# Second pass of a down projection: other places for a norm's chain, for gate weights and for embedding loads

## The chip, the core and the metric

One core of a Trainium2 chip runs the whole program. The metric is the device time of one execution in microseconds; the time before is the median of three runs, 795.0 us (793.97 to 795.13). The engines are TensorE (PE, which multiplies matrices), VectorE (DVE), ScalarE (ACT), GpSimd (POOL), and SyncE, whose queue (SP) issues the loads. Each engine takes its instructions in the order in which they were laid down for it.

## The reference

One layer of a hybrid model on 512 tokens of width 1024, in float32: a state-space mixer and a sparse attention side by side, their merge, a convolutional feed-forward block, a gated per-layer embedding, and a final norm. What matters here is the end:

```python
h = h + conv_ffn(rmsnorm(h, g_ffn[i]), w_up[i], conv_w[i], conv_b[i], w_down[i])
gate = jax.nn.sigmoid(rmsnorm(h, g_ple[i]) @ w_ple_gate[i])
h = h + gate * (p[i] @ w_ple_proj[i])
return rmsnorm(h, g_final)
```

`conv_ffn` ends in a product of a hidden 512 x 2816 with `w_down`, 2816 x 1024: the down projection. `rmsnorm(h, g_ple)` is called norm 3 below. `p @ w_ple_proj`, the embedding, does not depend on the rest; the kernel computes it at its start and parks it in DRAM (`pjd`), in eight pieces of 128 tokens by 512 columns.

## The kernel before

**Products.** Every float32 operand of a product is split into a high and a low part in a reduced format (`split`: ACT copies the high part, DVE or POOL subtracts it from the source to get the low one), and each product is three matmuls, high x high, high x low and low x high (`mm3`, lines 82 to 84).

**The down projection.** The hidden's 22 blocks of 128 rows are taken in 11 pairs. Pair 0 is done plainly. Pairs 1 to 10 (`for c in range(NR, NP)`) go through a scheme with seven half-size products in place of eight: the tokens are cut into halves of 256, the output into halves of 512 columns, and sums of weight blocks and of hidden blocks are multiplied. A *first pass* over the ten pairs does products 2, 1, 6 and 5. A *second pass* does product 3, two pairs at a time (`third(0)` to `third(4)`, twelve matmuls each), and then, per pair, products 4 and 7 (`fourth(c)`, twelve matmuls). The results are added onto the residual `hres` by DVE (`onto`). `sums_c(c)` loads sums of weights that were parked in DRAM (`ue`, 512 KB), and ACT and DVE split them into `uh`, `ul`, which have four places: pair c + 4 takes that of pair c once `fourth(c)` is done. `split_sums(1)` splits a pair's hidden sums for `fourth`.

**What else stands in the second pass.** `third(4)` completes product 3, so that DVE can complete the first 256 tokens of `hres`. These get norm 3 there: `squared_half` (ACT, sums of squares), `normed(0)` (ten small DVE operations that take the reciprocal root, then the scaling into `xn` on DVE and ACT), and `transposed(0, ...)`, a generator of two steps: each does eight transposes on PE, four copies on ACT (high parts `n`) and four operations on DVE (low parts `n`, line 63). The gate's weights are loaded and split as well: `gate_part(c)` for the first 512 output columns (`wg0`), `other_gate(c)` for the second (`wg1`), each c a fourth of the 1024 rows, 512 KB. `embedding(i)` loads the four parked pieces of column half i into `pj`.

**The gate** follows: eight groups of 24 matmuls into `pg`, in the order of tokens (0, 1) for column half 0, then half 1, then tokens (2, 3) for half 0 and half 1. The second token half's norm (`normed(1)`) is written at the end of the second pass, its two steps of transposes stand before the third and the fourth group. `sgt` is the tanh of a group and `gated_sum` puts gate and embedding onto `hres`. `g4` is the final gain, loaded and then scaled by POOL.

**Order.** In the second pass, up to `written.close()` (line 1841), the order of PE, SP, ACT and DVE is the order of the code. Behind it PE and SP keep the code's order and the others are ordered by a planner that simulates the program.

**Buffers.** Tiles come from `Slot`: 18 small ones of 512 columns (S0 to S17) and 22 big ones of 1024 (B0 to B21), in two lists of free slots. A new tile takes the slot that has been free longest; its first writer waits until the last reader of the tile that had the slot is done. `done()` puts a slot back. When no small slot is free, a big one is cut in two. Besides, `wraw` without a place of its own takes a buffer from a ring of three (tag `wr`), which the raw weights of the first pass, of `third` and of the gate share:

```python
if raw is None:
    raw = pw.tile([P, kt * c], F32, name="wr", tag="wr", bufs=3)
```

The second pass before the change, cut to its order:

```python
for c in range(NR, NP):
    if c == NR + 1:
        third(4)
        turned = transposed(0, normed(0, sns[0]))
    if c >= NP - 2:
        next(turned)
    fourth(c)
    n = c - NR
```

Of the kernel before, what the change touches and what calls it, by code (L numbers as in the profile page):

```python
# [18 lines left out]
P = 128  # L19
T = 512  # L20
NQ = T // P
D = 1024
# [22 lines left out]
def hybrid_kernel(ctx: ExitStack, tc: tile.TileContext, A, out):  # L45
# [3 lines left out]
    def dr(name, off, ap):  # L49
        t = A[name]  # L50
        return bass.AP(tensor=t.tensor, offset=t.offset + off, ap=ap)

    def tt(o, a, b, op, e=V):
        e.tensor_tensor(o, a, b, op=op)  # L54
# [19 lines left out]
    def copy(o, a):  # L74
        S.activation(o, a, AF.Copy)  # L75

    def split(hi, lo, src, e=V):
        copy(hi, src)
        tt(lo, src, hi, SUB, e)
# [20 lines left out]
    def bank(tag, name):  # L100
        return psp.tile([P, 512], F32, tag=tag, name=name, bufs=BANKS[tag])
# [80 lines left out]
    def wraw(name, ld, row0, c0, kt, c, raw=None):  # L182

        if raw is None:
            raw = pw.tile([P, kt * c], F32, name="wr", tag="wr", bufs=3)
            raw = raw.rearrange("p (k c) -> p k c", k=kt)
        n = (row0 // (kt * P)) * (ld // c) + c0 // c
        nc.sync.dma_start(raw, dr(name, n * P * kt * c, [[kt * c, P], [c, kt], [1, c]]))
        return raw

    def wload(name, ld, row0, c0, kt, c, e=V, keep=None, raw=None):
        if raw is None:
            raw = wraw(name, ld, row0, c0, kt, c)
        if keep is None:
            hi = pw.tile([P, kt * c], F32R, name="wh", tag="wh").rearrange("p (k c) -> p k c", k=kt)
            lo = pw.tile([P, kt * c], F32R, name="wl", tag="wl").rearrange("p (k c) -> p k c", k=kt)
        else:
            hi, lo = keep
        split(hi, lo, raw, e)
        return hi, lo  # L200
# [507 lines left out]
    for lv in range(5):  # L708
        n = 1 << lv
# [33 lines left out]
    with tc.issue_after(zero_at):  # L743
        for t in (*ZZ[0], *CX[0], *ZZ[1], *CX[1]):
            n = t.shape[1] * t.shape[2] * t.shape[3] * t.shape[4] // 8
# [297 lines left out]
    for hc in range(2):  # L1043
# [3 lines left out]
        for cc in range(2):  # L1047
            c = 2 * hc + cc
# [15 lines left out]
    class Unit:  # L1064
# [40 lines left out]
        def transposed(self, kt):  # L1105
            w = T - kt * P
            ps = bank("t", "ptp")
            for qt in range(kt, NQ):
                PE.transpose(ps[:, (qt - kt) * P:(qt - kt + 1) * P],  # L1109
                             self.pr[qt][:, kt * P:(kt + 1) * P], ident)  # L1110
            self.ph[kt], self.pl[kt] = (pt.tile([P, T], F32R, name=n, tag=n, bufs=3)[:, :w] for n in ("ph", "pl"))
            split(self.ph[kt], self.pl[kt], ps[:, :w])
# [331 lines left out]
    NP = NF // 2  # L1444
    NR = 1
# [102 lines left out]
    def sums_split(c, n, x):  # L1548
        t = Slot("ue", 2)
        nc.sync.dma_start(t.parts(), sums[c][2 * n:2 * n + 2].rearrange("n p c -> p n c"))  # L1550
        split(uh[:, x], ul[:, x], t.parts())
        t.done()

    park_at = [2, 4, 6, 8, 9, 11, 13, 14, 16, 18]
    for f in range(NF):
# [6 lines left out]
        for ab in range(2):  # L1562
            keep = [kept[2 * ab + x].parts(KD) for x in range(2)] if kept else None
# [22 lines left out]
    with tc.manual_schedule(engines={mybir.EngineType.PE, mybir.EngineType.SP}):  # L1586
# [7 lines left out]
        def sums_c(c):  # L1594
            sums_split(c, 1, (c - NP) % NSET)
# [45 lines left out]
        def product(n, c, lhs, rhs, js=(0, 1)):  # L1641
            for j in js:
                x = slice(j * P, (j + 1) * P)
                mm3(acc[n][j], lhs[0][:, x], lhs[1][:, x], rhs[0], rhs[1], c == NR and n != 2, c == NP - 1, n == 2)
# [6 lines left out]

        n3w = 2

        def gate_part(c):

            raw = wraw("w_ple_gate", D, 2 * c * P, 0, 2, 512)
            for k in range(2):
                wg0.append([Slot(f"wg0{x}", 1, F32R).t for x in "hl"])
                split(*wg0[-1], raw[:, k])

        def embedding(i):

            for qt in range(NQ):
                pjs[i, qt] = Slot("pj", 1).t
                nc.sync.dma_start(pjs[i, qt], pjd[i, qt])

# [62 lines left out]
        def third(x):  # L1729
            w, own = third_w.pop(x)  # L1730
            for i, c in enumerate(thirds[x]):
                product(3, c, hid[c].S4, (w[0][:, i], w[1][:, i]))
                for t in hid[c].split14:
                    t.done()
            for t in own:
                t.done()
# [11 lines left out]
        def squared_half(qp, sn, i, js=(0, 1)):  # L1748
            for j in js:
                S.activation(pw.tile([P, 512], F32, name="sq", tag="mg"), halves(hres[:, 2 * qp + j])[i], AF.Square,  # L1750
                             accum_out=sn[:, 2 * i + j:2 * i + j + 1])
# [4 lines left out]
        def normed(qp, sn):  # L1756
            xns = [[Slot("xn", 1) for _ in range(2)] for _ in range(2)]
            tt(sn[:, 0:2], sn[:, 0:2], sn[:, 2:4], ADD)
            r = rstd_of(sn[:, 0:2], n=2)
            for j in range(2):  # L1760
                scaled([t.t for t in xns[j]], halves(hres[:, 2 * qp + j]), r[:, j:j + 1])
            return xns
# [25 lines left out]
        sns = [sn_of(0), sn_of(1)]  # L1788
        wg1 = []

        def other_gate(c):
            wg1.append([Slot(f"wg1{x}", 2, F32R).parts() for x in "hl"])
            wload("w_ple_gate", D, 2 * c * P, 512, 2, 512, keep=wg1[-1])

        squared_half(0, sns[0], 0)
        third(0)
        third_weights(3)
        third(1)
# [4 lines left out]
        third_weights(4)  # L1803
        third(2)
        third(3)
        sums_c(NR + 3)
        for j in range(2):
            onto(j, D1, u5s[:, j])
        hid[NP - 4].split_sums(1)
        for c in range(NR, NP):  # L1810
            if c == NR + 1:
                third(4)
                for j in range(2):
                    onto(j, D1, acc[3][j])
                squared_half(0, sns[0], 1)
                for j in range(2):
                    onto(2 + j, D0, u2s[:, j])
                    onto(2 + j, D1, u5s[:, j])
                u2.done()
                u5.done()  # L1820
                turned = transposed(0, normed(0, sns[0]))
            if c >= NP - 2:
                next(turned)
            fourth(c)
            n = c - NR
            if c + 4 < NP:
                sums_c(c + 4)
            if n == 0:
                gate_part(1)
                other_gate(0)  # L1830
                other_gate(1)
            if n < 3:
                hid[NP - 3 + n].split_sums(1)
            if n in (3, 5):
                gate_part(2 + (n - 3) // 2)
            if n in (4, 6):
                embedding((n - 4) // 2)
                other_gate(n // 2)
        WG.append(lambda x, k: wg0[k][x])
        turned = transposed(1, normed(1, sns[1]))  # L1840
        written.close()
        WG.append(lambda x, k: wg1[k // 2][x][:, k % 2])

# [1 line left out]
        sg4 = Slot("g4", 2)  # L1845
        g4 = sg4.t
        nc.sync.dma_start(g4, dr("g_final", 0, [[0, P], [1, D]]))
        sgs = [Slot("sgt", 1) for _ in range(2)]
        sgn = [0]
        ts(g4, g4, math.sqrt(D), e=G)  # L1850
        ss = [pf.tile([P, 8], F32, name=f"ssf{qt}") for qt in range(NQ)]
# [163 lines left out]
```

## Time and profile before

| | |
|---|---|
| median of the runs | 795.0 us (793.97 to 795.13) |
| profiled execution: its time | 795.69 us |
| its span, first to last instruction | 794.0 us |
| PE busy | 777.7 us, 98% of the span |
| DVE, ACT, POOL busy | 563.5, 416.5, 250.1 us |
| PE clock granted, mean | 0.995 |

In rows of the trace the columns are start, duration, engine, line, operation, output<-inputs, shapes and count; in brackets stands how long the engine had been idle before and what released it. A row with a count over one merges neighbours of one kind. SP rows are the issuing of loads; the time from there until the data is in place is called landing. Names are those of buffers, and where two tiles shared a buffer, one can be shown under the other's name (`wg0l` for a hidden sum, `pj` for an `xn`). Matmul rows overlap, so PE's pace is read from start to start.

### The profile page before, as it was taken

How to read it: one execution, taken by the hardware profiler on the slowest of the kernel's cores; microseconds unless marked ns; L12 is line 12 of the kernel's file. 1: busy time of each engine (PE TensorE's matmuls, PEld its weight loads, DVE VectorE, ACT ScalarE, POOL GpSimd, SP SyncE). 2: the span in 40 equal slices, each digit the busy share in tenths (PEclk: the TensorE clock that was granted, in tenths of full speed). 3: DMA queues.
4: the chain of work that ended last, by engine and by line, in shares of the span. 5: the costliest groups of instructions: out<-in, count | busy, mean ns of one | idle time of the engine just before them, and what ended most of it. 6: DMA issues, size and time to landing. Idle time of an engine off the chain costs nothing.

```text
span 794.0 us, 12256 instructions
## 1 busy us (share of the span) xinstructions
PE 777.7 (98%) x4404; PEld 655.7 (83%) x4404; DVE 563.5 (71%) x1137; ACT 416.5 (52%) x757; POOL 250.1 (32%) x298
## 2 busy tenths in 40 slices
PE   9999999999999999999999999999999999999896
PEld 8887878888888888888998888888888888887685
DVE  6987999766677639798675566665664776876743
ACT  6836645657777654445644344344344446645532
POOL 3577433136465534001123332333332300000221
PEclk9999999999999999999999999999999999999899
DMA  8954121423234136201155566566544275576011
GB/s 345 362 158 148 60 88 47 141 72 114 55 107 157 56 125 247 96 11 54 36 189 200 206 206 229 186 237 209 194 151 133 106 273 207 172 280 209 0 54 54
DMA packets 44333, 118.59 MB, mean 149 GB/s; under 512 B 5360, under 2 KB 7792, under 8 KB 44272
## 3 DMA queue, kind: packets, MB, share of 16 engines
q1 hardware_dynamic: 43696, 116.75, 43.0%
q10 hardware_dynamic: 576, 1.05, 0.4%
q8 instruction: 35, 0.57, 0.3%
q14 instruction: 26, 0.21, 0.1%
HBM read 97.86 MB, written 15.73 MB: 143 GB/s over the span
## 4 chain that ended last, share of the span: by engine, by line
PE 89%; DVE 6%; ACT 2%; issue 2%; DMA 1%; POOL 0%; POOLq 0%; ACTq 0%; SPq 0%; DVEq 0%
PE pj L82 6%; PE pj L83 5%; PE pj L84 5%; PE ua L83 5%; PE ua L82 5%; PE ub L83 5%; PE ub L82 5%; PE ua L84 5%; PE ub L84 5%; PE p L84 3%; PE p L82 3%; PE p L83 3%; PE sps L1089 2%; PE ptp L1109 2%; PE br L82 2%; PE br L84 2%
## 5 line engine op out<-in xcount | busy, mean ns | idle before, releaser
L54 POOL TENSOR_TENSOR wl<-wr,wh 128x1024 fp32r<-128x1024 f32 x45 | 109.6, 2435 | 285.8 <-ACT wh L75 279.0
L75 ACT ACTIVATE wh<-wr 128x1024 fp32r<-128x1024 f32 x96 | 101.4, 1057 | 91.0 <-issue 34.8
L82 PE MATMUL pj<-n1h,wh 128*128 128x512 f32 x224 | 90.9, 406 | 0.4 <-DVE QT L54 0.4
L83 PE MATMUL pj<-n1l,wh 128*128 128x512 f32 x224 | 87.9, 392 | 0.0
L84 PE MATMUL pj<-n1h,wl 128*128 128x512 f32 x224 | 87.7, 392 | 0.0
L54 DVE TENSOR_TENSOR wl<-wr,wh 128x1024 fp32r<-128x1024 f32 x51 | 62.8, 1231 | 32.7 <-ACT wh L75 32.7
L63 DVE SCALAR_TENSOR_TENSOR cv<-ub,cols,cv 128x511 f32<-128x511 f32 (+1 forms) x44 | 33.0, 749 | 48.1 <-ACT cv L1511 47.3
L83 PE MATMUL ua<-n2l,wh 128*128 128x512 f32 (+1 forms) x168 | 64.6, 385 | 0.0
L82 PE MATMUL ua<-n2h,wh 128*128 128x512 f32 (+1 forms) x168 | 64.6, 385 | 0.0
L84 PE MATMUL ua<-n2h,wl 128*128 128x512 f32 (+1 forms) x168 | 64.5, 384 | 0.0
L84 PE MATMUL ub<-n2h,wl 128*128 128x512 f32 (+1 forms) x168 | 64.5, 384 | 0.0
L82 PE MATMUL ub<-n2h,wh 128*128 128x512 f32 (+1 forms) x168 | 64.5, 384 | 0.0
L83 PE MATMUL ub<-n2l,wh 128*128 128x512 f32 (+1 forms) x168 | 64.5, 384 | 0.0
L84 PEld LDWEIGHTS pj<-n1h,wl 128*128 128x128 f32 x224 | 42.1, 188 | 8.9
L82 PEld LDWEIGHTS pj<-n1h,wh 128*128 128x128 f32 x224 | 42.1, 188 | 8.3 <-DVE QT L54 0.9
L83 PEld LDWEIGHTS pj<-n1l,wh 128*128 128x128 f32 x224 | 42.2, 188 | 7.4 <-issue 0.2
L60 POOL TENSOR_SCALAR pr<-pr,su,gates 128x512 f32<-128x512 f32 (+2 forms) x64 | 38.7, 616 | 16.5 <-DVE su L1101 16.1
L75 ACT ACTIVATE ph<-ptp 128x128 fp32r<-128x128 f32 (+1 forms) x64 | 27.9, 436 | 26.1 <-PE ptp L1109 25.9
L54 DVE TENSOR_TENSOR pl<-ptp,ph 128x128 fp32r<-128x128 f32 (+1 forms) x64 | 31.1, 486 | 14.3 <-ACT ph L75 13.3
L1100 ACT ACTIVATE pr<-pr,nb 128x512 f32<-128x512 f32 (+2 forms) x64 | 35.5, 558 | 3.0 <-DVE nb L1098 2.9
L82 PEld LDWEIGHTS ub<-n2h,wh 128*128 128x128 f32 x168 | 31.6, 188 | 6.3
L84 PEld LDWEIGHTS ua<-n2h,wl 128*128 128x128 f32 x168 | 31.6, 188 | 6.3
(499 smaller groups left out, 2036.1 us busy)
## 6 DMA issues: line engine op xcount, KB each, us to landing
wr<-in_w_up_dram SPq DMA_DIRECT2D x44, 512.0 KB, 3.8
wr<-in_w_in_dram SPq DMA_DIRECT2D x28, 512.0 KB, 4.0
b<-in_w_down_dram SPq DMA_DIRECT2D x20, 512.0 KB, 5.5
bs<-b SPq DMA_DIRECT2D x40, 256.0 KB, 3.1
ue<-bs SPq DMA_DIRECT2D x20, 512.0 KB, 5.2
wr<-in_w_down_dram SPq DMA_DIRECT2D x12, 512.0 KB, 4.0
QQ<-QT SPq DMA_DIRECT2D x16, 256.0 KB, 4.6
xs<-in_w_out_dram SPq DMA_DIRECT2D x8, 512.0 KB, 8.3
```

What stands on the lines that cost most here:

```text
L54: e.tensor_tensor(o, a, b, op=op)
L60: e.tensor_scalar(o, a, s1, s2, op0=op0, op1=op1)
L63: e.scalar_tensor_tensor(o, a, s, b, op0=op0, op1=op1)
L75: S.activation(o, a, AF.Copy)
L82: PE.matmul(ps, lh, rh, start=start, stop=False, skip_group_check=goes_on)
L83: PE.matmul(ps, lh, rl, start=False, stop=False, skip_group_check=goes_on)
L84: PE.matmul(ps, ll, rh, start=False, stop=stop, skip_group_check=goes_on)
L1089: PE.matmul(o, self.QQ[:, x, qt * P:(qt + 1) * P], KK[:, :, self.g, :w] if both else KK[:, self.br, self.g, :w], start=x == 0, stop=x == 1)
L1100: S.activation(pp, pp, AF.Exp, bias=nb, scale=-1.0, accum_out=su)
L1109: PE.transpose(ps[:, (qt - kt) * P:(qt - kt + 1) * P], self.pr[qt][:, kt * P:(kt + 1) * P], ident)
```

## The change

Raw gate weights get slots of their own (`gate_raw`, one big slot each, given back after the split) in place of the ring. `gate_part(1)` and `other_gate(0)` move ahead of the loop over `fourth`; `other_gate(1)` stays in step 0; `normed(0)` moves from step 1, ahead of `fourth(2)`, to the end of step 2; the first `squared_half` moves behind `third(3)`; `other_gate(2)` moves from step 4 to step 6 and `other_gate(3)` from step 6 to step 8, behind the first step of transposes and `fourth(9)`. Of the eight embedding loads, two stay in the pass (step 6, behind `other_gate(2)`), six go behind `normed(1)`, ahead of the final gain's load. The two `sgt` slots are taken earlier, ahead of those six.

```diff
+        def gate_raw(c, i):
+            s_ = Slot("gr", 2)
+            return s_, wraw("w_ple_gate", D, 2 * c * P, i * 512, 2, 512, raw=s_.parts())
+
         def gate_part(c):
-
-            raw = wraw("w_ple_gate", D, 2 * c * P, 0, 2, 512)
+            s_, raw = gate_raw(c, 0)
             for k in range(2):
                 wg0.append([Slot(f"wg0{x}", 1, F32R).t for x in "hl"])
                 split(*wg0[-1], raw[:, k])
-
-        def embedding(i):
-
-            for qt in range(NQ):
+            s_.done()
+
+        def embedding(i, qts):
+
+            for qt in qts:
                 pjs[i, qt] = Slot("pj", 1).t
                 nc.sync.dma_start(pjs[i, qt], pjd[i, qt])
...
         def other_gate(c):
+            s_, raw = gate_raw(c, 1)
             wg1.append([Slot(f"wg1{x}", 2, F32R).parts() for x in "hl"])
-            wload("w_ple_gate", D, 2 * c * P, 512, 2, 512, keep=wg1[-1])
-
-        squared_half(0, sns[0], 0)
+            split(*wg1[-1], raw)
+            s_.done()
+
         third(0)
         third_weights(3)
...
         third(2)
         third(3)
+        squared_half(0, sns[0], 0)
+        gate_part(1)
         sums_c(NR + 3)
+        other_gate(0)
...
-        for c in range(NR, NP):
-            if c == NR + 1:
+        for n, c in enumerate(range(NR, NP)):
+            if n == 1:
                 third(4)
...
-                turned = transposed(0, normed(0, sns[0]))
             if c >= NP - 2:
                 next(turned)
             fourth(c)
-            n = c - NR
             if c + 4 < NP:
                 sums_c(c + 4)
-            if n == 0:
-                gate_part(1)
-                other_gate(0)
-                other_gate(1)
             if n < 3:
                 hid[NP - 3 + n].split_sums(1)
+            if n == 0:
+                other_gate(1)
+            if n == 2:
+                turned = transposed(0, normed(0, sns[0]))
             if n in (3, 5):
                 gate_part(2 + (n - 3) // 2)
-            if n in (4, 6):
-                embedding((n - 4) // 2)
-                other_gate(n // 2)
+            if n == 6:
+                other_gate(2)
+                embedding(0, range(2))
+            if n == 8:
+                other_gate(3)
         WG.append(lambda x, k: wg0[k][x])
         turned = transposed(1, normed(1, sns[1]))
+        sgs = [Slot("sgt", 1) for _ in range(2)]
+        embedding(1, range(2))
+        for i in range(2):
+            embedding(i, range(2, NQ))
         written.close()
```

More of the change, by code (lines that the diff above doesn't have):

```diff
@@ L1847, in hybrid_kernel @@
         nc.sync.dma_start(g4, dr("g_final", 0, [[0, P], [1, D]]))
-        sgs = [Slot("sgt", 1) for _ in range(2)]
         sgn = [0]
```

## The prediction

> **What bounds the kernel now.** I read the page's engine shares, then all waits of TensorE (PE), then the last hundred microseconds in stretches, then the instructions of PE, ScalarE (ACT), VectorE (DVE) and the DMA queue (SP) in order of time around the two places that came up. First the page's share and the longest wait of PE in the whole execution (total, times, longest):
>
> ```profile
> PE 777.7 (98%) x4404; PEld 655.7 (83%) x4404; DVE 563.5 (71%) x1137; ACT 416.5 (52%) x757; POOL 250.1 (32%) x298
> ...
> PE pg L82 <- DVE n L63: 3.5, 1, 3.5
> ```
>
> PE is busy 98% of the span, so time can come back only where PE waits or runs slowly. The longest wait is for the second pass's follower, the gate (`pg`). Stretches of time around it (length; busy time and instructions of PE, its weight loads, DVE, ACT and POOL; PE clock, DMA share, GB/s):
>
> ```profile
> 734.71:738.41 3.70, 0.16 (x2) 0.03 (x1) 3.70 (x8) 2.86 (x8) 3.33 (x1) 0.90 0.00 0
> 738.41:744.73 6.32, 6.32 (x15) 5.00 (x16) 4.90 (x11) 2.67 (x8) 0.14 (x1) 0.52 0.00 0
> ```
>
> Behind the second pass PE stands for 3.70 us, and then runs 6.3 us at a clock of 0.52. No DMA moves then. PE's own instructions:
>
> ```profile
> 714.54 0.39 PE L82 MATMUL p<-uh,ffsh 128*128 128x512 f32 x1
> ...
> 717.03 0.39 PE L84 MATMUL p<-uh,ffsh 128*128 128x512 f32 x1
> 718.08 0.50 PE L82 MATMUL p<-uh,wg0l 128*128 128x512 f32 x1 [0.66 <-ACT uh L75]
> 719.34 0.50 PE L83 MATMUL p<-ul,wg0l 128*128 128x512 f32 x1 [0.76 <-DVE ul L54]
> 719.68 0.40 PE L84 MATMUL p<-uh,ffsl 128*128 128x512 f32 x1
> ...
> 724.73 0.39 PE L82 MATMUL p<-uh,ffsh 128*128 128x512 f32 x1
> ...
> 734.48 0.39 PE L84 MATMUL p<-uh,ffsl 128*128 128x512 f32 x1
> 738.41 0.77 PE L82 MATMUL pg<-wg0h,n 128*128 128x512 f32 x1 [3.54 <-DVE n L63]
> ...
> 744.50 0.40 PE L84 MATMUL pg<-wg0h,n 128*128 128x512 f32 x1
> ```
>
> From 714.54 to 717.03 are eleven steps, 0.226 us each: full rate. Call `fourth(c)` f(c); each is twelve steps, 2.72 us. f(6)'s third matmul was due at 717.26 + 0.45 = 717.71 and ran at 719.68: **1.97 us lost**. The gate's first matmul was due at 734.71 and ran at 738.41: **3.70 lost**. The next fourteen steps, to 744.50, took 6.09 instead of 3.17: **2.92 lost**. Together 8.59 us that the change could return; elsewhere in the pass PE keeps its pace.
>
> Why PE waited, on ACT (four rows), DVE (three) and SP (two):
>
> ```profile
> 715.74 1.34 ACT L148 ACTIVATE xn<-hres,ry 128x512 f32<-128x512 f32 x2 [3.46 <-DVE ry L63]
> 716.99 1.04 ACT L75 ACTIVATE uh<-ue 128x1024 fp32r<-128x1024 f32 x1
> ...
> 733.59 1.06 ACT L75 ACTIVATE wg1h<-wr 128x1024 fp32r<-128x1024 f32 x1 [7.69 <-DMA wr<-in_w_ple_gate_dram]
> 734.56 3.01 ACT L169 ACTIVATE n<-nt,cols 128x256 fp32r<-128x256 f32 x8
> ...
> 711.37 2.49 DVE L54 TENSOR_TENSOR hres<-hres,u 128x512 f32<-128x512 f32 x4
> 713.78 0.15 DVE L54 TENSOR_TENSOR ssn<-ssn 128x2 f32<-128x2 f32 x1
> ...
> 735.83 3.22 DVE L63 SCALAR_TENSOR_TENSOR n<-nt,cols,n 128x256 fp32r<-128x256 f32 x8
> ...
> 724.92 2.78 SPq L1665 DMA_DIRECT2D pj<-pjd  x4
> 727.80 0.38 SPq L188 DMA_DIRECT2D wr<-in_w_ple_gate_dram  x1
> ```
>
> First place: f(6)'s high part `uh` (716.99) stands on ACT behind `normed(0)`'s `xn`, which waited 3.46 us for the norm's chain on DVE. Second place: `other_gate(3)`'s split waited 7.69 us for its load, and all eight copies `n` of norm 3's transposed rows stood behind it. The load left SP only at 727.80, behind four embedding loads. PE went on 0.13 us after the sixth low part (735.83 + 6 x 0.40 = 738.28).
>
> **The change, part by part.** All times below are on the clock of before; without the first stall each f starts 1.97 earlier: f(8) at 724.73 - 1.97 = 722.76, f(7) 2.72 before it at 720.04, the end of the pass E at 734.71 - 1.97 = 732.74. f(10) starts 2.72 before that, at 730.0; two groups of transposes share the 1.8 left between the end of f(8) and f(10) beside f(9), which starts at 726.4.
>
> *Norm 3's chain, one step later.* No instruction is added. On ACT and DVE the order becomes: the adds after `third(4)`, two squares, the split for f(6), that of hidden pair 9, f(7), pair 10, then the chain, then f(8). `gate_part(1)` and `other_gate(0)` now stand ahead of the loop, where DVE had idled 3.37 us; their work, 1.2 us each on DVE, is covered by that hole. Only one gate split is left ahead of the adds.
>
> ```profile
> 704.95 1.23 DVE L54 TENSOR_TENSOR ul<-ue,uh 128x1024 fp32r<-128x1024 f32 x1 [3.37 <-ACT uh L75]
> 706.10 1.28 DVE L54 TENSOR_TENSOR wg0l<-wr,wg0h 128x512 fp32r<-128x512 f32 x2
> 707.30 2.35 DVE L54 TENSOR_TENSOR wg1l<-wr,wg1h 128x1024 fp32r<-128x1024 f32 x2
> 710.17 1.28 DVE L54 TENSOR_TENSOR hres<-hres,p 128x512 f32<-128x512 f32 x2
> ...
> 710.95 0.63 ACT L1750 ACTIVATE sq<-hres 128x512 f32<-128x512 f32 x1 [2.57 <-DVE hres L54]
> ```
>
> So the adds start at 710.17 - 1.20 - 1.17 = 707.8. The squares began 0.8 behind them and take two times 0.66: 709.9. `uh`(6), 1.05, is done at 711.0; DVE is free of its adds at 707.8 + 1.2 + 2.5 = 711.5, `ul`(6), 1.2, done at 712.7, wanted at 717.26: 4.5 in hand. Pair 9 (0.6) and `ul`(7) to 714.5, wanted at 720.04. Pair 10 to 715.1, the chain's ten small operations (713.78 to 715.74 before) to 717.1, `xn` 1.3 to 718.4, `uh`(8) 719.4, `ul`(8) 720.6, wanted 722.76: 2.1 in hand, the tightest; f(9) has 3. So this part returns the 1.97.
>
> *Own slots for the raw gate weights.* The same loads of the same size; what each waits for I get by walking the lists of free slots through the code. The load of the sums for f(6) now waits for f(4)'s split, that for f(7) for `other_gate(0)`'s, that for f(8) for pair 7's. Where these end follows from ACT's last split ahead of the loop and the landings of the sums:
>
> ```profile
> 695.70 1.06 ACT L75 ACTIVATE wh<-wr 128x1024 fp32r<-128x1024 f32 x1 [1.61 <-PE p L84]
> ...
> DMA to landing us min/median/max: 3.6/6.5/7.8
> ```
>
> Behind 696.7 ACT has two squares (1.3), `gate_part(1)` (1.2) and `uh`(4) (1.0), and DVE its 1.2 after that: 701.3; `other_gate(0)` 1.2 more, 702.6; two adds and pair 7's part, 1.9, 704.5. Were `gate_part(1)`'s load late, f(4)'s split would be too, which has until 711.82. With the longest landing, 7.8, the three loads are there at 709.1, 710.4 and 712.3; ACT wants them at 709.9, after f(3) (711.8) and at 718.4. No cost; were one late, f(6) to f(8) would wait by what goes beyond the room above. Gate groups 2 and 3 and `other_gate(2)` are there long before use. In the first pass only `gate_part(0)`'s load leaves the ring of three; it comes sooner.
>
> *Two embedding loads and the last gate group.* `embedding(0, ...)`'s first two slots are those of pair 7's sums, so SP holds until f(7) is done. Before, SP issued its first one 0.42 after f(7)'s last matmul started (724.50, by the step of 0.226; 724.92); now at 720.04 + 11 x 0.226 + 0.42 = 722.95. Issues are (2.78 - 0.9)/4 = 0.47 apart, 0.9 of the 2.78 being a wait. `other_gate(3)` goes at 723.9, not 727.80. Its landing:
>
> ```profile
> SPq L1665 <- DVE wg1l L54: 0.9, 1, 0.9
> ...
> wr<-in_w_ple_gate_dram SPq DMA_DIRECT2D x1, 512.0 KB, 5.8
> g<-in_g_final_dram SPq DMA_DIRECT2D x1, 512.0 KB, 6.6
> ...
> DMA to landing us min/median/max: 2.6/3.7/7.7
> ```
>
> 5.8 was with 1 MB ahead of it; half of that is ahead now. I take 5.0, between the median 3.7 of these weight loads and 5.8: 728.9. ACT's split to 730.0, DVE's to 731.2; by then the first half of the transposed rows has been copied, which is the other thing the move does. The second half is transposed by 730.0; its two low parts that free PE's bank, 0.40 each behind DVE's split, end at 732.0, and E is 732.74. So 0.7 in hand: the stall of 3.70 and, with it, the slow stretch of 2.92 go. At the longest landing, 7.7, the bank is free at 734.7: a stall of 2.0.
>
> Whether 2.0 would slow PE's clock: the waits at 717 to 719, 1.05 and 1.26 from start to start, left the next step at 0.23, the one of 3.9 did not. The Trainium skill (TensorE: The Clock Gate, "What's actually happening") has the clock halved after an idle window of about 3.4 us; by it this stall would stay at full rate. It also has a busy window of about 3.4 us bring it back; our row says 6.09, and the row is used.
>
> *Six embedding loads and the final gain behind the pass.* They wait for f(10), go from E + 0.2 at 0.47 apart, so the gain goes at E + 3.0 and lands by E + 9.6 (6.6 above); six embedding loads need to be there only for the third gate group and later, from E + 16 on. On PE nothing waits for the gain, but GpSimd (POOL) scales it, and that may meet the second norm:
>
> ```profile
> 744.28 0.17 DVE L60 TENSOR_SCALAR ry<-rv 128x2 int32<-128x2 int32 x1
> 747.62 0.69 DVE L63 SCALAR_TENSOR_TENSOR sgt<-sgt,pj 128x512 f32<-128x512 f32 x1 [3.17 <-ACT sgt L1866]
> ...
> 750.13 1.46 DVE L58 TENSOR_SCALAR pj<-hres,ry 128x512 f32<-128x512 f32 x1
> 751.51 0.47 DVE L58 TENSOR_SCALAR xn<-hres,ry 128x512 f32<-128x512 f32 x1
> ...
> 746.99 0.60 ACT L1866 ACTIVATE sgt<-pg 128x512 f32<-128x512 f32 x1 [3.15 <-PE pg L84]
> ...
> 735.08 3.47 POOL L58 TENSOR_SCALAR g<-g 128x1024 f32<-128x1024 f32 x1 [104.34 <-DMA g<-in_g_final_dram]
> 750.00 1.30 POOL L54 TENSOR_TENSOR hres<-hres,g 128x512 f32<-128x512 f32 x1 [11.46 <-ACT sq L1875]
> ```
>
> `normed(1)` ended at 751.51 + 0.47 = 751.98, 5.0 after PE's first gate group ended and ACT's tanh began (746.99); the second group takes 24 x 0.226 = 5.4, so its transposes were in time by 0.4, and are again. One `xn` took 1.46 instead of 0.47 while POOL worked. If POOL's 3.47 falls there instead, it ends up to 3.47 - 0.99 = 2.5 later, less 0.4: 0 to 2.1 us. If it doesn't, the 0.99 is gone, which PE does not feel. I take 0.4.
>
> The Trainium skill (SBUF — State Buffer, "SBUF: two separate sides") calls the port pair of VectorE and GpSimd an exclusive lock for a whole instruction; for the one `xn` the trace agrees (1.46). By it the chain's two-input steps would wait as well, so that scaling anywhere in the chain's last 3.5 us would take the full 2.1 from the sum.
>
> **Sum.** 8.59 - 0.4 = 8.2 off the profiled execution: span 794.0 to 785.8. That execution took 795.69, its span and 1.7 around it, and becomes 787.5; the runs shown have a median of 795.0, 0.7 less, so **786.8 us**.
>
> **Rivals.**
> (1) The last gate load lands late and the wait before the gate stays in part: 2.0, or 4.9 if the slow stretch follows: 788.4 to 791.3. For it: ACT and DVE are still in order, and the load still stands behind two that wait for f(7). Against: it begins only 0.7 beyond the landing I take, and 2.0 needs 2.7 beyond.
> (2) POOL's scaling sits on the second norm: 2.1, 788.5. For it, 1.46 against 0.47; against, it needs the gain to land within about a microsecond of `xn`.
> (3) Slower. After the pass ACT and DVE are ordered by the planner, which before already put the first gate group's `sgt` (747.62) between `ry` (744.28) and the rest of its chain. Were it to put the second group's two steps ahead as well, the chain would go on after E + 10.9 (two groups) + 0.6 (746.99 to 747.62) + 1.4, and need 1.4 for seven small steps, 1.9 for `xn` (1.46 + 0.47) and 0.3 to PE: E + 16.5, where PE wants it at E + 10.9. 5.6 lost and 2.92 at the slow clock: 786.8 + 8.5 = 795.3, and 797.4 with POOL's 2.1 in the same place. It decides if one step of group two stands ahead of `rt`. Against it: the chain's next step is ready 5 us before that group ends.
> (4) The change doesn't do what it says: the gate's start hangs on ACT's and DVE's work in the pass as a whole, and PE, sooner at f(6), waits longer behind f(10): 794.5 to 795.0. Against it: ACT idled 7.69 us in that stretch.
>
> **How the numbers follow.** Forecast 0.70 (785.8 to 787.5), (1) 0.12, (2) 0.06, (3) 0.08, (4) 0.04. The range 785.7 to 791.3 holds the forecast, (1) and (2). About 0.2% (1.6 us) can be told from no change here. Faster: 0.70 + 0.12 + 0.06 = 0.88; slower: the part of (3) above 796.6, 0.05; within 0.2%: the rest of (3) and (4), 0.07.
>
> **What would show it.** Right: no wait of PE before `pg`'s first matmul, its steps at 0.23 from the start; f(6) without wait; `xn` on ACT behind `uh` for f(7); the last gate load issued about 9 us before the pass ends. Wrong: a wait of PE on `n` or `nt`, a PE clock under 1 around the start of the gate, or a new wait of an `uh` or `ul` on its load.

## The result and the profile after

The changed kernel takes **786.52 us** (median of 786.5 to 786.87), against 794.56 us (793.97 to 795.13) for the kernel before, timed beside it. The ratio is 0.990, 95% interval 0.9883 to 0.9917. That is 8.0 us less; 8.2 less and 786.8 us were forecast. The profiled execution's span went from 794.0 to 784.8 us.

The page's shares, and the waits of PE in the whole execution after the change (total, times, longest):

```profile
PE 773.7 (99%) x4404; PEld 653.1 (83%) x4404; DVE 565.1 (72%) x1137; ACT 416.6 (53%) x757; POOL 251.1 (32%) x298
```

```profile
PE yps L870 <- DVE sr L54: 2.0, 2, 1.2
PE warm L456 <- DVE heat L241: 1.1, 1, 1.1
PE yps L872 <- ACT tz L75: 0.8, 1, 0.8
PE pj L82 <- DVE QT L54: 0.4, 1, 0.4
```

The wait of 3.5 us at `pg`, the longest one before, is gone from the list, and so are those of `p`. What is left lies in the first 200 us of the program. PE in order of time, at f(6), at the end of the pass and at the gate:

```profile
716.76 0.39 PE L82 MATMUL p<-uh,wg0l 128*128 128x512 f32 x1
716.98 0.39 PE L83 MATMUL p<-ul,wg0l 128*128 128x512 f32 x1
...
731.95 0.39 PE L84 MATMUL p<-uh,ffsl 128*128 128x512 f32 x1
732.18 0.39 PE L82 MATMUL pg<-wg0h,n 128*128 128x512 f32 x1
...
735.35 0.39 PE L84 MATMUL pg<-wg0h,n 128*128 128x512 f32 x1
...
743.06 1.03 PE L166 MATMUL nt<-ident,xn 128*128 128x128 f32 x8
```

f(6)'s rows stand 0.22 apart with no wait in brackets. The gate's first matmul starts 0.23 after the last of f(10), and the next fourteen steps take 735.35 - 732.18 = 3.17 us, where they took 6.09. The second norm's transposes (743.06) have no wait either. The clock in that stretch (length; busy PE, PEld, DVE, ACT, POOL; PE clock, DMA share, GB/s):

```profile
732.18:738.50 6.32, 6.32 (x29) 5.26 (x28) 4.63 (x14) 3.27 (x9) 0.00 (x0) 1.00 0.82 271
```

1.00, against 0.52 in the 6.32 us behind the wait before.

So all three losses were returned, 1.97 + 3.70 + 2.92 = 8.59 us. The span fell by 9.2, and 0.50 of the rest has nothing to do with the change: PE comes to f(6) at 716.76 and not 717.26, because PE ran earlier almost from the start of the program on: by 0.41 us in the row below, and by 0.50 from some 120 us on. In the profiles of the kernels shown here, which do the same work there, this row starts anywhere between 16.38 and 17.56. Before and after:

```profile
17.55 1.19 PE L300 MATMUL vps<-WV,n1h 128*128 128x280 f32 x8
```

```profile
17.14 1.29 PE L300 MATMUL vps<-WV,n1h 128*128 128x280 f32 x8
```

Times of after are therefore 0.50 us earlier than the prediction's clock; where the two are compared below, 0.50 is added.

ScalarE, VectorE, SP and POOL of the changed kernel, in the rows that answer to the prediction's steps:

```profile
701.33 1.06 ACT L75 ACTIVATE wg1h<-gr 128x1024 fp32r<-128x1024 f32 x1 [1.72 <-DMA gr<-in_w_ple_gate_dram]
710.27 1.05 ACT L75 ACTIVATE uh<-ue 128x1024 fp32r<-128x1024 f32 x1
717.30 1.34 ACT L148 ACTIVATE xn<-hres,ry 128x512 f32<-128x512 f32 x2 [3.99 <-DVE ry L63]
727.96 1.06 ACT L75 ACTIVATE wg1h<-gr 128x1024 fp32r<-128x1024 f32 x1 [0.83 <-DMA gr<-in_w_ple_gate_dram]
```

```profile
708.25 1.28 DVE L54 TENSOR_TENSOR hres<-hres,p 128x512 f32<-128x512 f32 x2
711.85 1.22 DVE L54 TENSOR_TENSOR ul<-ue,uh 128x1024 fp32r<-128x1024 f32 x1
719.62 1.23 DVE L54 TENSOR_TENSOR ul<-ue,uh 128x1024 fp32r<-128x1024 f32 x1 [1.44 <-ACT uh L75]
730.19 1.65 DVE L63 SCALAR_TENSOR_TENSOR n<-nt,cols,n 128x256 fp32r<-128x256 f32 x4
731.76 4.06 DVE L54 TENSOR_TENSOR hres<-hres,p 128x512 f32<-128x512 f32 x6
740.17 1.66 DVE L58 TENSOR_SCALAR xn<-hres,ry 128x512 f32<-128x512 f32 x2
```

```profile
722.16 0.80 SPq L1669 DMA_DIRECT2D pj<-pjd  x2
723.07 1.57 SPq L188 DMA_DIRECT2D gr<-in_w_ple_gate_dram  x1
732.14 2.69 SPq L1669 DMA_DIRECT2D pj<-pjd  x6
734.93 0.38 SPq L1859 DMA_DIRECT2D g<-in_g_final_dram  x1
```

```profile
gr<-in_w_ple_gate_dram SPq DMA_DIRECT2D x1, 512.0 KB, 4.8
g<-in_g_final_dram SPq DMA_DIRECT2D x1, 512.0 KB, 5.4
```

`xn` (717.30) now stands on ACT behind the splits for f(6) and f(7). The last gate load leaves SP at 723.07, behind two embedding loads, and the other six (732.14) follow the pass.

### The profile page after: what moved, and what is told of

Read it like the earlier page. It is cut to its first block, busy times and chain, and to the rows that moved or that the text cites. A ratio compares the mean times of both kernels' runs of the same rounds, so it can differ in the third digit from the quotient of the medians.

```text
span 784.8 us, 12266 instructions
## 1 busy us (share of the span) xinstructions
PE 773.7 (99%) x4404; PEld 653.1 (83%) x4404; DVE 565.1 (72%) x1137; ACT 416.6 (53%) x757; POOL 251.1 (32%) x298
## 4 chain that ended last, share of the span: by engine, by line
PE 87%; DVE 5%; DMA 3%; ACT 2%; issue 1%; SPq 1%; POOL 0%; POOLq 0%; ACTq 0%; DVEq 0%
PE ua L83 5%; PE ua L84 5%; PE ub L84 5%; PE ub L83 5%; PE ua L82 5%; PE ub L82 5%; PE pj L82 5%; PE pj L83 5%; PE pj L84 5%; PE p L83 3%; PE p L82 3%; PE p L84 3%; PE sps L1089 2%; PE ptp L1109 2%; PE br L82 2%; PE br L83 2%
## 5 line engine op out<-in xcount | busy, mean ns | idle before, releaser
L58 POOL TENSOR_SCALAR g<-g 128x1024 f32<-128x1024 f32 x1 | 2.8, 2810 | 110.2 <-DMA g<-in_g_final_dram 110.2
L83 PEld LDWEIGHTS ub<-n2l,wh 128*128 128x128 f32 x168 | 31.6, 188 | 6.3
```

The costliest lines, as they stand in the source:

```text
L58: e.tensor_scalar(o, a, s1, None, op0=op0)
L83: PE.matmul(ps, lh, rl, start=False, stop=False, skip_group_check=goes_on)
```

## The experiments

The change does several things at once, and two of them could each have freed f(6), two of them the gate. Six kernels start from before and make parts of the change; three start from the changed kernel and take a part back or move the gain; three put embedding loads back ahead of the last gate load, to find the price of lateness. Where waits are named, they are PE's in the profiled execution.

**Norm 3's chain alone** (norm_only): before, with `normed(0)` at the end of step 2.

```diff
             if c == NR + 1:
...
-                turned = transposed(0, normed(0, sns[0]))
...
+            if n == 2:
+                turned = transposed(0, normed(0, sns[0]))
```

> The kernel before with one edit: norm 3's chain is written at the end of step 2 instead of step 1; gate weights, embedding loads and the ring stay. Theory A (the losses are separate): f(6)'s 1.97 us return, the last gate load still stands behind the four embedding loads that wait for f(7), so the wait before the gate and the slow stretch stay as they are, moved 2 us earlier: 794.6 - 2.0 = 792.6. Rival B (ACT's and DVE's work in the pass sets the gate's start): PE waits 2 us longer before the gate, 794.6.

Measured: 790.79 us (789.25 to 790.84), ratio 0.9955 (0.9939 to 0.9972). f(6) has no wait. The gate's wait stays, at 3.04 us by the bracket where it was 3.54 (from leaving SP to ACT's split the last gate load takes 4.7 us here and took 5.8 before), with a slow stretch behind it:

```profile
734.76 0.47 PE L82 MATMUL pg<-wg0h,n 128*128 128x512 f32 x1 [3.04 <-DVE n L63]
...
735.33 0.63 PE L84 MATMUL pg<-wg0h,n 128*128 128x512 f32 x1
...
739.64 0.39 PE L84 MATMUL pg<-wg0h,n 128*128 128x512 f32 x1
```

Fourteen steps take 739.64 - 734.76 = 4.88 us, 1.71 more than at full rate. The chain's move by itself returns what is lost at f(6), and not what is lost at the gate. That the gate's loss would stay as large as it was didn't come out.

**Two gate groups ahead of the loop alone** (gates_early): before, with `gate_part(1)` and `other_gate(0)` ahead of the loop, and the first `squared_half` behind `third(3)`.

```diff
-        squared_half(0, sns[0], 0)
         third(0)
...
         third(3)
+        squared_half(0, sns[0], 0)
+        gate_part(1)
         sums_c(NR + 3)
+        other_gate(0)
...
-            if n == 0:
-                gate_part(1)
-                other_gate(0)
-                other_gate(1)
...
```

(`other_gate(1)` stays in step 0, behind `split_sums`.)

> The kernel before with gate_part(1) and other_gate(0) ahead of the loop (and the first squares behind third(3)), raw weights still in the ring, norm 3's chain and the embedding loads where they were. Theory A: the adds that open the chain come 1.9 us earlier on DVE, so that f(6)'s second matmul is late by only 0.4 instead of 1.97; the wait before the gate stays: 794.6 - 1.5 = 793.1. Rival: only the place of the chain matters for f(6): 794.6.

Measured: 790.35 us (789.14 to 792.26), ratio 0.9958 (0.9943 to 0.9974). f(6) has no wait here either, with the chain still ahead of its split; the 0.4 us that was expected isn't there. The gate's wait, and PE's step behind it:

```profile
734.71 0.47 PE L82 MATMUL pg<-wg0h,n 128*128 128x512 f32 x1 [2.28 <-DVE n L63]
735.02 0.40 PE L83 MATMUL pg<-wg0l,n 128*128 128x512 f32 x1
```

So for f(6) either of the two moves is enough. After this wait of 2.28 us PE's first step takes 0.31, and the next ones 0.23, the full rate, in the profiled execution (789.14 us, mean clock 0.998). The slowest execution of the same kernel took 792.26 us at a mean clock of 0.996.

**Four embedding loads behind the pass alone** (embed_only): before, with the second column half's four loads behind `normed(1)`, and the `sgt` slots taken ahead of them.

```diff
             if n in (4, 6):
-                embedding((n - 4) // 2)
+                if n == 4:
+                    embedding(0)
                 other_gate(n // 2)
...
         turned = transposed(1, normed(1, sns[1]))
+        sgs = [Slot("sgt", 1) for _ in range(2)]
+        embedding(1)
...
```

> The kernel before with the second four embedding loads behind normed(1) (and the two tanh slots taken ahead of them); everything else as before. Theory A: the last gate load is issued some 7 us earlier, right behind the load of gate group 3, and lands before ACT wants it: the wait of 3.70 and the slow stretch of 2.92 go, f(6)'s wait stays: 794.6 - 6.6 = 788.0. Rival B: the wait before the gate stays, 794.6.

Measured: 788.53 us (788.09 to 789.06), ratio 0.9933 (0.9919 to 0.9948). What is left are the two waits at f(6), the same as before:

```profile
717.31 0.50 PE L82 MATMUL p<-uh,wg0l 128*128 128x512 f32 x1 [0.66 <-ACT uh L75]
718.57 0.51 PE L83 MATMUL p<-ul,wg0l 128*128 128x512 f32 x1 [0.76 <-DVE ul L54]
```

The gate has no wait, though `other_gate(3)` still stands in step 6, ahead of both transpose steps. So its move to step 8 isn't what frees the gate; taking the embedding loads from ahead of its load is. PE comes to the gate 1.97 us later here than in the changed kernel, which helps; gates_and_embed below has the gate free without that.

**Chain and embedding loads together** (norm_and_embed): the edits of norm_only and embed_only in one kernel.

```diff
-                turned = transposed(0, normed(0, sns[0]))
...
+            if n == 2:
+                turned = transposed(0, normed(0, sns[0]))
...
-                embedding((n - 4) // 2)
+                if n == 4:
+                    embedding(0)
...
+        embedding(1)
...
```

> The two edits together on the kernel before: the chain at the end of step 2 and the second four embedding loads behind normed(1). Gate weights still in the ring and at their old places. Theory A: all three losses go, as with the whole change: 786.5, and no wait of PE from 690 us to the end. Rival: own slots or the gate groups' new places are needed too, and it stays 1 us or more above 786.5.

Measured: 788.22 us (787.98 to 788.76), ratio 0.993 (0.9915 to 0.9945). f(6) and the gate are free, and a new wait stands before the second norm's transposes. PE, then POOL, then DVE:

```profile
744.81 0.98 PE L166 MATMUL nt<-ident,xn 128*128 128x128 f32 x7 [0.93 <-DVE xn L58]
```

```profile
740.26 2.80 POOL L58 TENSOR_SCALAR g<-g 128x1024 f32<-128x1024 f32 x1 [109.52 <-DMA g<-in_g_final_dram]
743.14 1.33 POOL L54 TENSOR_TENSOR hres<-hres,g 128x512 f32<-128x512 f32 x1
```

```profile
740.33 0.99 DVE L54 TENSOR_TENSOR rt<-rt,rv 128x2 f32<-128x2 f32 x1
742.34 2.42 DVE L58 TENSOR_SCALAR xn<-hres,ry 128x512 f32<-128x512 f32 x2
```

This is the mechanism of rival (2) in a sister kernel. POOL scales the gain from 740.26; `rt`, else 0.16 us, takes 0.99. Then POOL's product holds the pair of `xn`, which takes 2.42 us and ends at 744.76, 0.29 after POOL.

**The same with the gain's load four loads sooner** (norm_embed_gain): the kernel of norm_and_embed, with the final gain's load ahead of the four late embedding loads and not behind them.

```diff
         sgs = [Slot("sgt", 1) for _ in range(2)]
+        sg4 = Slot("g4", 2)
+        g4 = sg4.t
+        nc.sync.dma_start(g4, dr("g_final", 0, [[0, P], [1, D]]))
         embedding(1)
...
```

> This is the kernel of norm_and_embed (before, with norm 3's chain at the end of step 2 and the second four embedding loads behind `normed(1)`), with one edit more: the final gain's load goes ahead of those four embedding loads. Theory: the new wait of 0.93 us before the second norm's transposes in norm_and_embed is POOL's doing, whose scaling of the gain (740.26 to 743.06) and first product with it (743.14 to 744.47) lay on the second norm's last steps. Four loads at 0.47 less ahead of it, the scaling begins some 1.9 us sooner, near 738.4 in norm_and_embed's clock, and has passed before `xn` (742.34). Then `xn` takes 0.88 for two, PE doesn't wait, and the time is 788.2 - 0.9 = 787.3 us or a little above. Rival: the chain itself is late there, because the last gate load's split stands before both transpose steps (chain 1.2 us later than in the changed kernel), and POOL has little part in it: then the wait stays at 0.6 or more, and the time at 787.9 to 788.2 us.

Measured: 786.75 us (786.62 to 787.02), ratio 0.9905 (0.9886 to 0.9923). The wait is gone. The gain's load doesn't wait for the pass to end as the embedding's do, so POOL scales at 730.16, much sooner than expected, and only its product (741.33) still meets `xn`:

```profile
730.16 2.78 POOL L58 TENSOR_SCALAR g<-g 128x1024 f32<-128x1024 f32 x1 [100.10 <-PE p L84]
```

```profile
741.46 1.85 DVE L58 TENSOR_SCALAR xn<-hres,ry 128x512 f32<-128x512 f32 x2
```

```profile
732.58 0.47 PE L82 MATMUL pg<-wg0h,n 128*128 128x512 f32 x1 [0.38 <-DVE n L63]
...
743.57 1.03 PE L166 MATMUL nt<-ident,xn 128*128 128x128 f32 x8
```

It confirms that POOL's scaling made the wait, and the late chain alone did not: the chain's first small step comes 5.5 us after the gate's first matmul here (738.06 and 732.58) and came 5.2 after it there (737.89 and 732.72). What this kernel still has is a wait of 0.38 at the gate. The last gate load takes 4.4 us from leaving SP to ACT's split, where it took 3.6 in norm_and_embed; that the gain's load, now right behind it, slows it is likely and not shown.

**The smallest pair** (gates_and_embed): the edits of gates_early and embed_only; chain, ring and last gate groups as before.

```diff
+        gate_part(1)
         sums_c(NR + 3)
+        other_gate(0)
...
-                embedding((n - 4) // 2)
+                if n == 4:
+                    embedding(0)
...
+        embedding(1)
...
```

> Before, with two edits: `gate_part(1)` and `other_gate(0)` ahead of the loop (the first `squared_half` behind `third(3)`), and the second four embedding loads behind `normed(1)`. The norm's chain stays in step 1, raw weights stay in the ring, the last gate groups stay in steps 4 and 6. Theory: these two edits remove all of the 8.59 us (f(6) without wait as in gates_early, the gate without wait as in embed_only); what can be left is the wait of about 0.9 before the second norm's transposes that norm_and_embed has, because here as there PE is 2 us sooner at the gate, the last gate group's split stands before both transpose steps, and the gain's load leaves at the same place. So one wait of 0.5 to 1.0 on `xn`, and 787.3 to 788.2 us. Rival A: the whole change's other parts aren't needed at all: no wait, 786.5 to 786.9. Rival B: two early gate groups are not enough for f(6) once the embedding's slots are taken otherwise: f(6) waits 1 us or more, 788.3 and up.

Measured: 787.08 us (786.71 to 788.33), ratio 0.9912 (0.9889 to 0.9936). One wait is left, on `xn`, a third of the one in norm_and_embed:

```profile
743.66 0.98 PE L166 MATMUL nt<-ident,xn 128*128 128x128 f32 x7 [0.30 <-DVE xn L58]
```

```profile
731.68 4.05 DVE L54 TENSOR_TENSOR hres<-hres,p 128x512 f32<-128x512 f32 x6
...
739.21 1.49 DVE L63 SCALAR_TENSOR_TENSOR hres<-sgt,hres 128x512 f32<-128x512 f32 x1
...
741.00 2.61 DVE L58 TENSOR_SCALAR xn<-hres,ry 128x512 f32<-128x512 f32 x2
```

The reason expected for it isn't the one found. The chain is not late: its adds start at 731.68, as in the changed kernel (731.76), because the load of the last gate group, whose split still stands ahead of both transpose steps, is there in time. But the gain has two embedding loads fewer ahead of it than in the changed kernel, POOL scales at 739.09 and not 740.48, and holds first `hres` (1.49 instead of 0.69) and then, with its product, `xn`.

7.4 of the 8.0 us come from these two edits. What the rest of the change adds to them is about half a microsecond (0.56 between the medians, 0.52 between the profiles), and room.

**The chain back in step 1** (norm_back): the changed kernel without the chain's move.

```diff
+                turned = transposed(0, normed(0, sns[0]))
             if c >= NP - 2:
...
-            if n == 2:
-                turned = transposed(0, normed(0, sns[0]))
```

> The changed kernel with norm 3's chain back in step 1, ahead of fourth(2). Theory A with the trace of the changed kernel: there the adds that open the chain end at 711.94 instead of 713.86, so f(6)'s second matmul could start at 719.34 - 1.92 = 717.42, due 716.98: 0.44 us late, 786.5 + 0.4 = 786.9. Rival: the chain's place carries the whole 1.97: 788.5.

Measured: 786.69 us (786.05 to 787.32), ratio 0.9919 (0.99 to 0.9938), no wait. The low part for f(6) on DVE, and f(6):

```profile
715.08 1.23 DVE L54 TENSOR_TENSOR ul<-ue,uh 128x1024 fp32r<-128x1024 f32 x1 [1.43 <-ACT uh L75]
```

```profile
716.63 0.39 PE L82 MATMUL p<-uh,wg0l 128*128 128x512 f32 x1
```

The expected wait of 0.44 us isn't there. `ul`(6) is done at 716.31, 0.3 us before f(6) and 0.5 before the second matmul, the first that reads it. In the changed kernel it is done at 711.85 + 1.22 = 713.1, 3.7 before. So here the chain's move buys room, and no time. The room can matter: in this profile the adds start 0.9 us sooner than in the changed kernel's, because the load for `other_gate(0)` was there sooner (its split starts at 699.97, against 701.33 there). With that load as late as there, 0.5 would not have been enough.

**The raw weights back in the ring** (ring): `gate_raw` takes no slot, `wraw` uses the ring of three again.

```diff
         def gate_raw(c, i):
-            s_ = Slot("gr", 2)
-            return s_, wraw("w_ple_gate", D, 2 * c * P, i * 512, 2, 512, raw=s_.parts())
+            return wraw("w_ple_gate", D, 2 * c * P, i * 512, 2, 512)
...
```

> The changed kernel with the raw gate weights back in the ring of three, nothing else. Theory A: each gate load then waits for a split that ends 5 us or more before the load is needed, so nothing changes: 786.5. Rival: own slots are what lets the loads leave early, and a wait of PE on a gate's or a sum's split comes back: 787.5 or more.

Measured: 786.71 us (786.17 to 786.91), ratio 0.9919 (0.9897 to 0.9941), no wait in the pass or at the gate. Own slots bring nothing.

**The gain nearer to the pass** (gain_mid): the changed kernel with the gain's load behind the first two of the six late embedding loads.

```diff
         embedding(1, range(2))
+        sg4 = Slot("g4", 2)
+        g4 = sg4.t
+        nc.sync.dma_start(g4, dr("g_final", 0, [[0, P], [1, D]]))
         for i in range(2):
             embedding(i, range(2, NQ))
...
```

> The changed kernel with the final gain's load behind the first two of the six late embedding loads instead of behind all six. It then goes at about 733.0, lands near 737.9, and POOL scales it from there for 2.8 to 3.5 us, over the second norm's small steps and xn on DVE. Rival (2) of the prediction, a lock for whole instructions: DVE's steps stand until POOL is done, xn ends up to 2.8 later than 741.9, and PE's third group of transposes, at 743.06, waits up to 1.6: 786.5 to 788.1, with a hole of 1 us or more in DVE's chain. If the two engines share, the chain keeps its pace of 0.2 a step: 786.5.

Measured: 786.67 us (786.21 to 786.95), ratio 0.9919 (0.99 to 0.9937), no wait. POOL's scaling now lies on the norm's last small steps:

```profile
739.20 3.55 POOL L58 TENSOR_SCALAR g<-g 128x1024 f32<-128x1024 f32 x1 [109.00 <-DVE rt L54]
```

```profile
739.75 0.99 DVE L54 TENSOR_TENSOR rt<-rt,rv 128x2 f32<-128x2 f32 x1
740.97 0.88 DVE L58 TENSOR_SCALAR xn<-hres,ry 128x512 f32<-128x512 f32 x2
```

One `rt` is held for 0.83; both `xn` run at their usual pace while POOL's instruction still goes on to 742.75. So scaling within the chain costs the chain 0.8 and not POOL's whole duration.

**Four, six and eight embedding loads ahead of the last gate load** (four_ahead, six_ahead, eight_ahead): the changed kernel, with more of them in step 6 and fewer behind the pass.

```diff
-                embedding(0, range(2))
+                embedding(0, range(NQ))
...
-        embedding(1, range(2))
-        for i in range(2):
-            embedding(i, range(2, NQ))
+        embedding(1, range(NQ))
```

That is the kernel with four. With six, step 6 also has `embedding(1, range(2))` and behind the pass stands `embedding(1, range(2, NQ))`; with eight, step 6 has all and behind the pass stands none.

> The changed kernel with four instead of two embedding loads ahead of the last gate load. Issued 0.85 us later, with 1 MB ahead of it instead of 0.5: it lands near 729.7 instead of 727.96 (5.8 us, as before with the same four ahead). From landing to PE's first gate matmul the trace has 3.2 (ACT's split, DVE's split, two low parts): 732.9, due at 732.18: a wait of about 0.7 at the full clock behind it: 787.2. Rival: no wait, 786.5.

> The changed kernel with six embedding loads ahead of the last gate load. By the step from two to four it lands near 731.4 and PE waits about 2.4 before the gate. The question is the clock: if a wait under 3.4 us leaves it, as the clock page of the Trainium skill has it, 788.9; if any wait of that length brings the half-speed stretch of 2.9 with it, 791.8.

> The changed kernel with all eight embedding loads ahead of the last gate load. By the same steps it lands near 733.1, and PE waits about 4.1 before the gate, a little more than in the kernel before, with the slow stretch of 2.9 behind it: 793.5. If the wait is not what slows the clock: 790.6.

| loads ahead | load leaves SP | ACT's split starts | wait at the gate | time, us | ratio to before |
|---|---|---|---|---|---|
| 2 (the change) | 723.07 | 727.96 | 0 | 786.52 (786.5 to 786.87) | 0.990 (0.9883 to 0.9917) |
| 4 | 725.40 | 730.07 | 0.98 | 787.95 (787.37 to 788.25) | 0.9934 (0.9916 to 0.9953) |
| 6 | 726.64 | 731.47 | 1.93 | 789.37 (789.04 to 791.75) | 0.995 (0.9936 to 0.9964) |
| 8 | 727.32 | 733.18 | 4.10 | 792.46 (791.52 to 793.82) | 0.9987 (0.9973 to 1.0) |

The gate's first matmul with four, six and eight ahead:

```profile
733.32 0.47 PE L82 MATMUL pg<-wg0h,n 128*128 128x512 f32 x1 [0.98 <-DVE n L63]
```

```profile
734.72 0.47 PE L82 MATMUL pg<-wg0h,n 128*128 128x512 f32 x1 [1.93 <-DVE n L63]
```

```profile
736.43 0.77 PE L82 MATMUL pg<-wg0h,n 128*128 128x512 f32 x1 [4.10 <-DVE n L63]
...
741.03 0.40 PE L84 MATMUL pg<-wg0h,n 128*128 128x512 f32 x1
```

With four, six and eight ahead the split starts 2.11, 3.06 and 5.22 us later than in the changed kernel, and the gate's first matmul (732.18 there) 1.14, 2.09 and 4.25 later; for six, 0.45 is taken off, by which this execution is later throughout. The matmul is 0.97 less late than the split each time. (The wait in brackets counts from the end of the matmul before, which overlaps the next, and is 0.16 less than the lateness.) So the last gate load is on the path as soon as it is 1.0 us late, and from there each microsecond costs one. The kernel with eight pays more: its fourteen steps take 741.03 - 736.43 = 4.60 us, 1.43 more than at full rate. With eight ahead nearly the whole gain at the gate is lost, with everything else of the change in place.

The expected place of the split in four_ahead (729.7, measured 730.07) came out by two errors that cancel: the load left SP 2.33 us later and not 0.85, and took 4.7 us to land and not 5.8. In six_ahead the profiled execution keeps the full clock behind its wait, as the lower of its two expectations had it; in eight_ahead the slow stretch of 2.9 was expected, and half of it came.

No experiment has a lower median than the changed kernel.

## Why the prediction was right

**The three losses and their causes.** Right: f(6) and the gate run without wait and at full clock, and the sum of 8.59 is what PE got back. embed_only and norm_only each remove one of the two waits and leave the other, so they are two causes, and the slow stretch goes with the second.

**Norm 3's chain.** The order came out as written, each step 0.7 to 1.0 us later than worked out: the adds start at 708.25 + 0.50 = 708.75 (forecast 707.8), `ul`(6) is done at 713.6 (712.7), `ul`(8) at 721.35 (720.6), which leaves 1.4 in hand and not 2.1. The row at 701.33 is the reason: the split of `other_gate(0)` waited 1.72 us for its load, a wait that the prediction's sum doesn't have. four_ahead is the same kernel up to there, and in its profile the load was there sooner:

```profile
699.95 1.06 ACT L75 ACTIVATE wg1h<-gr 128x1024 fp32r<-128x1024 f32 x1 [0.23 <-DMA gr<-in_w_ple_gate_dram]
```

Its adds start at 707.33, which is 707.83 on the prediction's clock, as forecast. The wrong step is the credit: "So this part returns the 1.97" was said of the chain's move, with the gate groups' move as its helper. gates_early and norm_back show that the two gate groups alone return it, and norm_only that the chain alone does. Each covers for the other.

**Own slots.** Costed at nothing, and ring shows the same on the other side: they bring nothing.

**The last gate load.** The terms came out close: first embedding load at 722.16 + 0.50 = 722.66 (forecast 722.95), gate load at 723.57 (723.9), landing 4.8 (5.0), ACT's split done at 729.5 (730.0), DVE's at 730.8 (731.2), and E at 732.68 (732.74). The room came out as 1.0 (0.7). The landing was near in part by luck: it was argued from the 1 MB ahead of the load before and half of that now, but with 1 MB ahead it took 4.7 us from SP to the split in norm_only, gates_early and four_ahead, and 5.8 in before. And the prediction saw two helpers, the load's earlier issue and the first half of the copies ahead of its split; by embed_only and gates_and_embed the second isn't needed.

**The gain's scaling, 0.4.** This term was too large by all of it: PE loses nothing there. The gain landed at 734.93 + 5.4 = 740.3, E + 8.1, and its scaling held one `xn` (the pair takes 1.66 and not 0.88), which the second norm's room still covered.

**The rivals.** (1), a late gate load, didn't happen here; six_ahead and eight_ahead show its price: with a wait of 1.93 us 789.37, where 788.4 was worked out for 2.0 at full clock (some of its executions ran at a lower one), and 792.46 with 4.10. (2), POOL on the second norm: here the scaling held `xn` for 0.8 us and cost PE nothing; in norm_and_embed PE waited 0.93. Two things keep the cost away in the changed kernel: the chain's adds start 0.7 us sooner than in norm_and_embed (731.76 against 732.97, of which 0.5 is that execution's later start), for which, by gates_and_embed, the two early gate groups are enough; and the gain comes 1.4 us later than in gates_and_embed. The forecast foresaw neither; it reckoned with a gain at E + 9.6. (3), the planner's order, didn't happen: the second group's `sgt` comes at 743.89, on DVE, behind `xn`. (4) is refuted by the missing wait.

**The time.** 795.0 - 8.2 = 786.8 against 786.52. With the 0.4 left out, it would have been 786.4. That the two agree so closely is partly luck. The 8.59 holds for the profiled execution of before, one of its slower ones, and was taken off the median; beside norm_back, ring and gain_mid the kernel before had a median of 793.67, and these three, whose profiles have spans of 784.7 to 784.8 us like the changed kernel's, were 7.0 us faster.

## What to carry to other kernels

When PE waits for an in-order engine's copies, look for the instruction ahead of them that waits for a load, and then for what stands ahead of that load in its queue: here six transfers that nobody needed until 16 us behind the pass cost nearly 6 us (eight_ahead). Cheap work that can go into an idle stretch earlier should go there first, since it frees the same engines later; moving the dependent chain back as well then buys only room. Behind each wait that is fixed, count the room of the next one to tenths of a microsecond, and ask of work on other engines (here one scaling on POOL) whether it now falls into that room.

## What the runs showed of the hardware

**The slow clock behind a wait isn't a fixed price.** In profiles, waits of 1.93 and 2.28 us were followed by full rate but for one step of 0.31 in place of 0.23, one of 3.04 by 1.71 us lost, one of 3.54 by 2.92, one of 4.10 by only 1.43. (The prediction read the step behind the wait at 719.34 as 0.23; it is 0.34, and the ones after it 0.23.) Executions of one kernel differ likewise: six_ahead ran at 789.04 to 789.44 us in six of ten executions, with a mean clock of 0.998 to 0.999, and at 790.36 to 791.75 in three, with 0.996 to 0.997; before ran from 791.4 at 0.999 to 795.78 at 0.995. The four kernels without any wait in this part (the changed one, norm_back, ring and gain_mid) vary less, by 0.4 to 1.3 us (the most is norm_back, from 786.05 at 0.999 to 787.32 at 0.997). Only one execution of each was profiled, so where the others lost their time isn't shown. So 2.92 was one execution's value, and the forecast, made against that execution and then carried to the median, was closer than it had to be. The Trainium skill (TensorE: Matmul & The Clock Gate, "What's actually happening") says that the window over which activity is judged runs freely and that the number of slow matmuls differs from run to run; these rows agree. Its idle window of about 3.4 us is not a safe limit here, since in norm_only a wait of 3.04 by the bracket, 3.19 from the time at which the next matmul was due, was enough.

**What POOL holds up.** POOL's scaling of 128 x 1024 (2.8 to 3.6 us) held one DVE instruction by 0.8 us, whichever it was (a 128 x 2 `rt` in norm_and_embed and gain_mid, `hres` in gates_and_embed, an `xn` in the changed kernel), and then let DVE go on while it ran: in norm_and_embed the two-input `rt` at 741.95 took its usual 0.16, with the scaling on until 743.06. In norm_embed_gain it ran beside DVE's eight low parts `n`, which took 3.22 us as they do without it. Its product of two tensors, 128 x 512 (1.3 us), held `xn` until 0.29 after its own end. The Trainium skill (SBUF — State Buffer, "SBUF: two separate sides") has the shared ports locked for the whole instruction, between one of GpSimd and one of VectorE that reads two inputs from SBUF or runs in a mode with two ports; that fits the time for which the product held `xn`, and not the scaling. The low parts `n`, which read `nt` from PSUM, don't test it.
